# A decoder layer on one Trainium2 core: the value projection as two Strassen passes, with keys and queries projected first

## The chip, the cores and the metric

The kernel runs on one core of a Trainium2 chip. The core has a matrix engine (PE, with PEld for its weight loads), a vector engine (DVE), a scalar engine (ACT), a general engine (POOL) and a sequencer for transfers (SP). The metric is the device time of one execution in microseconds. The kernel before took 2018.26 us in the median of three runs (2017.77 to 2018.28).

## The reference

One layer of a decoder trunk, 512 tokens by 2048 features, all in float32, and a final norm:

```
h = rmsnorm(x, ln_mix)
sb_q, sb_k, sb_v, sw_q, sw_k, sw_v = split(h @ w_in)        # w_in: 2048 x 4608
sb_o = stick_breaking_attention(sb_q, sb_k, sb_v)           # 16 heads of 64, strictly causal
sw_o = sliding_window_sink_attention(sw_q, sw_k, sw_v, sinks, slopes)   # 16 query heads, 4 key heads, window 128
x = x + concat(rmsnorm(sb_o), rmsnorm(sw_o)) @ w_out
gate, up = split(rmsnorm(x, ln_ffn) @ w_gate_up)            # 2048 x 2*5632
x = x + (silu(gate) * up) @ w_down
return rmsnorm(x, ln_final)
```

Stick-breaking attention has no softmax. Its weight is exp(log sigmoid(z) + the sum of log sigmoid(-z') over the keys between), for keys before the query. The value projection sb_v is h (512 x 2048) times a 2048 x 1024 part of w_in.

## The kernel before

A float32 product is made of three matmuls of rounded operands (float32r): high by high, low by high and high by low, where the low part is what rounding left. So each weight tile that arrives is split into a high part (a copy on ACT, `whi`) and a low part (a subtraction on DVE, `wlo`), and so are the activations.

**The queue.** Everything up to the second output projection is made from one list, `queue`. An entry (slab) names its sources, a prep function and its matmuls in groups of three. `step()` (L226) runs one group; at group 2 of a slab it also loads the next two slabs and splits the next one. `drain(mark)` (L264) steps up to a mark. `pull(ns)` (L254) steps until a budget is used up: a group of three 512-column matmuls counts 648, one of three 256-column matmuls 324; what a pull lacks or has too much is carried to the next one in `carry`, which is never reset. `defer(n, fn)` calls a function n steps later. The slabs cost about the same: 8 groups of 648, or 16 of 324. Buffers for raw weights (`RAWB`) are three, for split weights two.

**The order.** The first 16 slabs are the value projection, `add_v(0)` and `add_v(1)`: two halves of 512 columns, each 8 slabs of two row blocks. While the first half runs, x arrives in 20 pieces; the slabs' prep transposes it (`h_make`, two row blocks of 128 features a slab) and splits it into `h_hi` and `h_lo`. The transposes write tile z, the first half's sums tiles m and o (two PSUM banks each), the second half's tile z (four banks). `x_squares` and `rstd1_make` form the norm's factor, which is applied as the sums leave PSUM; the values go to `vst`, split again.

Then come 32 slabs of stick-breaking queries and keys (`add_qk(u)` for eight pairs of heads, four slabs each), 8 slabs of window keys and first window queries (`C_SWK`, `C_SWQ`, kept in `kq`), and 4 of window values (`add_swv`). They are the fill of the stick-breaking stage: 66 iterations over 64 jobs (16 heads by four key blocks), in each of which the stage's own small matmuls alternate with three pulls of `SBFILL / 3`, where `SBFILL` is 30 slabs over 62. `sb_begin(h)` drains the queue up to the slabs of its pair of heads, three jobs ahead. The marks leave the last slab of the window values outside the loop (`sb_mark = swv_end - 1`), and what the loop left over is drained behind it. Within an iteration the jobs overlap: the logarithm of job j (three ACT instructions, L614 to L616), the suffix sums of job j-1 (matmuls L661 to L664), its exponential (L669), the copy of job j's high part (L624), and the weighted sum of job j-2 (L684, L685). The weighted sum of a head takes one of the two o banks and is folded on ACT and DVE (L511, L513); every second head its square is added on POOL (L520, L521). The two factors of the output norms are made by `sumsq_rstd`, which takes another o bank.

The window attention (16 jobs, 18 iterations) follows with 12 more query slabs, of which the first group uses the two o banks, and 16 slabs of the first output projection as its fill, one slab's worth per iteration.

**What orders instructions.** A planner places the instructions of each engine, in general by the program's order, but an instruction whose inputs are ready can be placed ahead of one that waits. Those called through `pV`, `pA`, `pG`, `pT` and `dma` stay in program order among themselves on their engine.

**The down projection**, much later, already runs as ten passes of Strassen's scheme in the variant of Winograd: `class Pass`, with seven block products instead of eight, each in two slots of 12 matmuls, POOL making the differences of weight blocks, ACT two copies of each (`hp` into PSUM for the subtraction, `whi`), DVE the low part and the sums out of PSUM. A table of slots, `plan`, says in which slot each load, sum and copy is issued.

## Time and profile before

| | |
|---|---|
| median of three runs | 2018.26 us |
| span of the profiled execution | 2015.3 us |
| its own time | not listed apart from the span |
| PE busy | 2002.2 us (99%) |
| DVE, ACT, POOL busy | 1453.2, 1455.7, 1031.9 us |
| PE's share of the chain that ended last | 97% |

A row of a group reads: line, engine, operation, tiles (out<-in), shapes, count, then busy time, mean duration of one in ns, and the engine's idle time before them with what ended it. Matmuls are pipelined, so their listed duration is longer than their spacing. A row of a timeline reads: start in us, duration, engine, line, operation, and how many are merged. A row of windows gives the stretch, its length, and for PE, PEld, DVE, ACT and POOL the busy time and count, then the granted clock of PE, the DMA share and GB/s.

### The profile page before, as it was taken

How to read it: one execution, taken by the hardware profiler on the slowest of the kernel's cores; microseconds unless marked ns; L12 is line 12 of the kernel's file. 1: busy time of each engine (PE TensorE's matmuls, PEld its weight loads, DVE VectorE, ACT ScalarE, POOL GpSimd, SP SyncE). 2: the span in 40 equal slices, each digit the busy share in tenths (PEclk: the TensorE clock that was granted, in tenths of full speed). 3: DMA queues.
4: the chain of work that ended last, by engine and by line, in shares of the span. 5: the costliest groups of instructions: out<-in, count | busy, mean ns of one | idle time of the engine just before them, and what ended most of it. 6: DMA issues, size and time to landing. Idle time of an engine off the chain costs nothing.

```text
span 2015.3 us, 29246 instructions
## 1 busy us (share of the span) xinstructions
PE 2002.2 (99%) x10412; PEld 1707.3 (85%) x10412; DVE 1453.2 (72%) x1968; ACT 1455.7 (72%) x2009; POOL 1031.9 (51%) x562
## 2 busy tenths in 40 slices
PE   9999999999999999999999999999999999999998
PEld 8888888898788888888888888888888888888886
DVE  4358888768963777777777777777777867767767
ACT  5347777657842477777777777777777788788787
POOL 0014444300100066766667666666766778878883
PEclk9999999999999999999999999999999999999999
DMA  5332222222343354453544535444454743533523
GB/s 192 92 93 65 64 66 71 63 84 67 103 147 114 120 157 125 111 141 101 136 116 120 137 101 140 112 124 132 104 141 106 266 157 111 180 128 106 175 86 115
DMA packets 286369, 240.23 MB, mean 119 GB/s; under 512 B 11024, under 2 KB 237392, under 8 KB 283792
## 3 DMA queue, kind: packets, MB, share of 16 engines
q1 hardware_dynamic: 285552, 235.71, 39.6%
q8 instruction: 82, 1.34, 0.3%
q0 software_dynamic: 288, 1.32, 0.2%
q10 hardware_dynamic: 384, 1.34, 0.2%
q14 instruction: 63, 0.52, 0.1%
HBM read 218.40 MB, written 19.92 MB: 118 GB/s over the span
## 4 chain that ended last, share of the span: by engine, by line
PE 97%; DVE 1%; ACT 1%; issue 0%; DVEq 0%; POOL 0%; ACTq 0%; POOLq 0%
PE o L118 34%; PE m L118 28%; PE m L390 4%; PE m L391 4%; PE m L392 4%; PE m L359 2%; PE m L358 2%; PE m L360 2%; PE o L360 2%; PE o L359 2%; PE o L358 2%; PE z L118 1%; PE z L359 1%; PE z L360 1%; PE z L358 1%; PE z L853 1%
## 5 line engine op out<-in xcount | busy, mean ns | idle before, releaser
L118 POOL TENSOR_TENSOR t<-raw,t 128x1024 f32<-128x1024 f32 x107 | 272.6, 2548 | 277.5 <-ACT hp L118 263.3
L118 DVE TENSOR_TENSOR wlo<-t,hp 128x1024 fp32r<-128x1024 f32 x235 | 286.5, 1219 | 172.3 <-PE o L118 107.5
L118 ACT ACTIVATE whi<-t 128x1024 fp32r<-128x1024 f32 x235 | 249.3, 1061 | 123.1 <-PE o L118 74.7
L118 PE MATMUL o<-hca,whi 128*128 128x512 f32 x880 | 307.5, 391 | 0.0
L118 POOL TENSOR_TENSOR t<-raw,raw 128x1024 f32<-128x1024 f32 x106 | 275.3, 2601 | 16.0 <-issue 10.3
L118 DVE TENSOR_TENSOR wlo<-raw,hp 128x1024 fp32r<-128x1024 f32 x175 | 213.6, 1221 | 81.3 <-issue 50.5
L118 ACT ACTIVATE whi<-raw 128x1024 fp32r<-128x1024 f32 (+1 forms) x177 | 187.1, 1057 | 99.8 <-PE m L118 72.0
L118 PE MATMUL o<-hca,wlo 128*128 128x256 f32 x880 | 244.0, 280 | 0.0
L118 ACT ACTIVATE hp<-t 128x1024 fp32r<-128x1024 f32 x235 | 236.9, 1008 | 0.0
L220 DVE TENSOR_TENSOR wlo<-raw,whi 128x1024 fp32r<-128x1024 f32 x103 | 126.5, 1228 | 137.7 <-ACT whi L219 135.0
L219 ACT ACTIVATE whi<-raw 128x1024 fp32r<-128x1024 f32 x103 | 108.7, 1056 | 152.2 <-PE o L360 75.4
L118 PEld LDWEIGHTS o<-hca,whi 128*128 128x128 f32 x880 | 164.2, 187 | 35.8
L118 PE MATMUL m<-hca,whi 128*128 128x512 f32 x528 | 186.3, 392 | 1.1 <-DVE hca L118 1.1
L118 ACT ACTIVATE hp<-raw 128x1024 fp32r<-128x1024 f32 x179 | 180.8, 1010 | 3.1 <-DVE wlo L118 2.2
L118 PEld LDWEIGHTS o<-hca,wlo 128*128 128x128 f32 x880 | 165.6, 189 | 0.4
L390 PE MATMUL m<-hhi,whi 128*128 128x512 f32 x384 | 156.3, 407 | 0.0
L391 PE MATMUL m<-hlo,whi 128*128 128x512 f32 x384 | 150.5, 392 | 0.0
L392 PE MATMUL m<-hhi,wlo 128*128 128x512 f32 x384 | 150.4, 392 | 0.0
L118 PE MATMUL m<-whi,dca 128*128 128x512 f32 x592 | 146.9, 389 | 0.0
L118 PE MATMUL o<-whi,dca 128*128 128x512 f32 x592 | 146.8, 389 | 0.0
L118 PE MATMUL m<-hca,wlo 128*128 128x256 f32 x528 | 146.3, 280 | 0.0
L118 PEld LDWEIGHTS o<-whi,dca 128*128 128x128 f32 x592 | 111.1, 188 | 23.1
(351 smaller groups left out, 5143.6 us busy)
## 6 DMA issues: line engine op xcount, KB each, us to landing
raw<-in_w_gate_up_dram SPq DMA_DIRECT2D x348, 256.0 KB, 5.2
raw<-in_w_down_dram SPq DMA_DIRECT2D x68, 512.0 KB, 4.8
raw<-in_w_in_dram SPq DMA_DIRECT2D x39, 512.0 KB, 3.5
raw<-in_w_in_dram SPq DMA_DIRECT2D x66, 256.0 KB, 3.3
raw<-in_w_out_dram SPq DMA_DIRECT2D x32, 512.0 KB, 3.8
aT<-w SPq DMA_DIRECT2D x44, 256.0 KB, 3.5
xd<-aT SPq DMA_DIRECT2D x10, 1024.0 KB, 7.1
rx<-in_w_down_dram SPq DMA_DIRECT2D x20, 512.0 KB, 5.7
```

The source lines that it names most:

```text
L118: return lambda *a, **k: tc.keep_in_program_order(fn(*a, **k))
L219: A.activation(out=hi, in_=raw, func=AF.Copy)
L220: V.tensor_tensor(out=lo, in0=raw, in1=f(hi), op=ALU.subtract)
L358: mm(o, lhsT=lh[:, sl], rhs=hi[:, j, :], start=first, stop=False, skip_group_check=halves)
L359: mm(o, lhsT=lh[:, sl], rhs=lo[:, j, :], start=False, stop=False, skip_group_check=halves)
L360: mm(o, lhsT=ll[:, sl], rhs=hi[:, j, :], start=False, stop=(k == nslab * a - 1), skip_group_check=halves)
L390: mm(o, lhsT=wh, rhs=xh, start=(k == 0), stop=False)
L391: mm(o, lhsT=wh, rhs=xl, start=False, stop=False)
L392: mm(o, lhsT=wl, rhs=xh, start=False, stop=(k == KT - 1))
L853: nc.tensor.transpose(out=pb[:, hh * P:(hh + 1) * P], in_=B.s[hh // 2][:, hh % 2, j * P:(j + 1) * P], identity=ident)
```

## The change

The value projection h (512 x 2048) times 2048 x 1024 is made by two passes of the seven-product scheme, one for each half of the 2048 features (16 row blocks; four blocks of h of 256 tokens by 512 features, four of the weights of 512 by 512). `class Block` takes over what the down passes' `Pass` did, and `ValuePass` derives from it. Each product sums into two banks; `take` adds them into `vacc` in SBUF. As left operands the products 1, 2 and 4 use the `h_hi` and `h_lo` that exist; for 7, 6, 5 and 3 combinations of h are formed, from `hf`, the sum of both parts, which POOL now makes in `h_make`. The forms `diff`, `s1`, `s2` and `s4` run on POOL, their high parts on ACT, their low parts on DVE.

The eight slabs of window keys and first window queries move to the front of the queue, where x arrives (`add_kq`: four m and o banks, each slab's weights as two pieces of 256 columns; in slab 0 four). The x row blocks are prepared in the order of `KTS`, the last ones a slab sooner. At slab 5 the phase's memory is handed to the value passes, whose first loads and sums are issued between the remaining groups (slots -6 to -1). After slot 27 come the slabs 8 to 10 of stick-breaking queries, and the values are scaled and split out of `vacc` in deferred steps. The stick-breaking stage keeps its rate of pulling, but the eight slabs are no longer in its queue. Before the first window scores the drain up to `smarks[0]`, which was zero, becomes a pull of 16000.

```diff
-    def open_phase(name, bufs):
+    def open_phase(name, bufs, **kw):
...
         if i == 0:
             for j in range(a):
-                dma(out=raw[:, j, :], in_=srcs[0][j * P:(j + 1) * P, :])
+                for k, src in enumerate(srcs):
+                    dma(out=raw[:, j, k * n:(k + 1) * n], in_=src[j * P:(j + 1) * P, :])
...
         split_scaled(pb, gcol[:, kt:kt + 1], h_hi[kt], h_lo[kt])
+        if kt % 4 == 0:
+            h8s.append((h8[0], h8[1]))
+            hf.append(v8.tile([P, 4, 512], F32, tag="v8", name="hf"))
+        pG.tensor_tensor(out=hf[kt // 4][:, kt % 4, :], in0=f(h_hi[kt]), in1=f(h_lo[kt]), op=ALU.add)
...
+    PD = ("1", "7", "6", "4", "5", "2", "3")
+    class Block(Weights):
+        def __init__(self, d, g, c0, u, fresh):
+            Weights.__init__(self)
+            self.d, self.g, self.c0, self.u, self.fresh = d, g, c0, u, fresh
+            self.raw, self.t, self.bank = {}, {}, {}
+        def difference(self, p, i, t):
+            a, b = {"7": ("22", "12"), "5": ("12", "11"), "6": ("22", "T5"), "4": ("21", "T6")}[p]
+            self.t[p, i] = t
+            pG.tensor_tensor(out=t, in0=self.raw[a, i], in1=self.t[b[1], i] if b[0] == "T" else self.raw[b, i],
+                             op=ALU.subtract)
+        def src(self, pi):
+            p, i = pi
+            return self.t[pi] if pi in self.t else self.raw[{"1": "11", "2": "21", "3": "22"}[p], i]
+        def product(self, pi):
+            p, i = pi
+            if i == 0 and p in "1752":
+                get = (pm, po)[(self.d + (p in "72")) % 2]
+                self.bank[p] = [get(), get()]
+            on = {"6": "1", "4": "7", "3": "5"}.get(p)
+            bk = self.bank[on or p]
+            hi, lo = self.hi.pop(pi), self.lo.pop(pi)
+            for half, w in ((0, hi), (1, hi), (0, lo)):
+                for e in range(2):
+                    for t in range(2):
+                        pT.matmul(bk[t], lhsT=self.left(p, 2 * i + e, half, t * P), rhs=w[:, e, :],
+                                  start=(on is None and i == 0 and half == 0 and w is hi and e == 0),
+                                  stop=(w is lo and e == 1), skip_group_check=True)
...
-    vst = [v8.tile([P, 16, P], F32R, tag="v8", name="vst") for _ in range(NT)]
+    vst = [None] * NT
-    def add_v(c):
...
+    KTS = ((), (2, 3), (4, 5), (6, 7), (8, 9, 10), (11, 12, 13), (14, 15), ())
...
+    def add_kq():
...
         def prep(s):
-            if c == 0:
-                h_make(2 * s)
-                h_make(2 * s + 1)
-                if s == 7:
-                    defer(1, lambda: [x_squares(k) for k in range(3)])
-                    defer(2, lambda: [x_squares(k) for k in range(3, 5)])
-                    defer(4, rstd1_make)
-                    defer(11, rstd1_rows)
-        add_tok(lambda s: win[s * 256:(s + 1) * 256, C_SBV + c * 512:C_SBV + (c + 1) * 512],
-                8, 2, 512, hT, lambda: four(1 - c), v_done, prep)
+            for kt in KTS[s]:
+                h_make(kt)
+            for c in {3: (0, 1), 5: (2,), 6: (3,)}.get(s, ()):
+                x_squares(c)
+        for s in range(8):
+            order = [(c, j) for c in range(4) for j in range(2)] if s == 7 else [(c, j) for j in range(2) for c in range(4)]
+            rows = slice(s * 256, (s + 1) * 256)
+            queue.append(dict(srcs=[win[rows, C_SWK:C_SWK + 256], win[rows, C_SWQ:C_SWQ + 256]], a=2, b=512, big=None,
+                              mms=[one(c, j, s) for c, j in order], post=None,
+                              pre=(lambda: bk.update(b=four(1))) if s == 0 else None, prep=lambda s=s: prep(s)))
...
+    class ValuePass(Block):
...
+    vp = [ValuePass(g) for g in range(2)]
+    for g in range(2):
+        b0, u = 14 * g, vp[g]
+        for k, q, i in ((-6, "12", 0), (-6, "22", 0), (-5, "11", 0), (-4, "12", 1), (-3, "22", 1), (-2, "11", 1),
+                        (0, "21", 0), (1, "21", 1)):
+            at_slot(b0 + k, "load", u.load, q, i)
+        for k, p, i in ((-3, "7", 0), (-2, "5", 0), (-1, "7", 1), (0, "5", 1), (1, "6", 0), (2, "6", 1),
+                        (3, "4", 0), (4, "4", 1)):
+            at_slot(b0 + k, "sum", u.sum, p, i)
+        for k, fn, *args in ((-5, u.diff), (-5, u.s1), (-4, u.s2), (-4, u.form, "7", "h"), (-3, u.form, "7", "l"),
+                             (0, u.form, "6", "h"), (1, u.form, "6", "l"), (4, u.form, "5", "h"), (5, u.form, "5", "l"),
+                             (5, u.s4), (7, u.form, "3", "h"), (8, u.form, "3", "l")):
+            at_slot(b0 + k, "late", fn, *args)
+        for k, p in enumerate(PD):
+            at_slot(b0 + 2 * k + 2, "take", u.take, p)
+    for k in range(3):
+        at_slot(14 + (7, 9, 11)[k], "late", vp[1].add_v, k, pG)
...
-    add_v(0)
-    add_v(1)
+    add_kq()
...
-    NV = len(queue)
-    drain(NV - 2)
-    open_phase("sbp", 1)
+    def drain_to(slab, group):
+        while pos[0] < slab or pos[1] < group:
+            step()
+    def value_slot(n):
+        run(n, "load")
+        run(n, "sum")
+        vof(n + 1, "to_hi")
+        vof(n + 1, "to_lo")
+        vof(n + 2, "to_hp")
+    drain_to(5, 3)
+    x_squares(4)
+    defer(4, rstd1_make)
+    open_phase("vp", 1, reuse_waits="tile")
+    for n in range(-6, 0):
+        if n == -2:
+            open_z("psv")
+        value_slot(n)
+        if n == -1:
+            vacc[:] = [o8.tile([P, 4, 512], F32, tag="o8", name="vacc") for _ in range(2)]
+            vu.append(phase[1].tile([P, 2, 512], F32, tag="vu", name="vu", bufs=1))
+        while pos[0] * 8 + pos[1] < 64 + 4 * (n + 1):
+            step()
+        run(n, "late")
     for u in range(8):
         add_qk(u)
-    def kq_done(c, pb):
-        if kq[0] is None:
-            kq[0] = const.tile([P, 4, 512], F32, tag="swv", name="kq")
-        k_evac(pb, kq[0][:, c, :])
-
-    add_feat(win, [(C_SWK, 256)], two_m, kq_done)
-    add_feat(win, [(C_SWQ, 256)], two_m, lambda c, pb: q_evac(pb, kq[0][:, 2 + c, :]))
+    for n in range(28):
+        value_slot(n)
+        if n == 24:
+            load(8)
+        if n == 27:
+            load(9)
+            split(8)
+        vof(n, "product")
+        run(n, "take")
+        run(n, "late")
+    run(28, "take")
+    open_z("psw")
+    def value_split(c, t):
+        if vst[t] is None:
+            vst[t] = v8.tile([P, 16, P], F32R, tag="v8", name="vst")
+        bv = vacc[c][:, t, :].rearrange("p (h d) -> p h d", d=HD)
+        split_scaled(bv, rs1["c"][:, t:t + 1], vst[t][:, c * 8:(c + 1) * 8, 0:HD],
+                     vst[t][:, c * 8:(c + 1) * 8, HD:P])
+    for t in (3, 2, 1, 0):
+        value_split(0, t)
+    def kq_scale():
+        for c in range(4):
+            (k_evac if c < 2 else q_evac)(kq[0][:, c, :], kq[0][:, c, :])
+    defer(3, rstd1_rows)
+    defer(8, lambda: [value_split(1, t) for t in (3, 2, 1, 0)])
+    defer(14, kq_scale)
+    open_phase("sbp", 1)
+    drain_to(11, 0)
+    oA = [o8.tile([P, 4, 512], F32, tag="o8", name="oA") for _ in range(2)]
     add_swv()
...
-    drain(smarks[0])
+    pull(16000.0)
     at(swa_scores, 0)
...
-    class Pass(Weights):
+    class Pass(Block):
...
-    nc = _bacc.Bacc("TRN2", target_bir_lowering=False, num_devices=1)
+    nc = _bacc.Bacc("TRN2", target_bir_lowering=False, num_devices=1, dynamic_dma_scratch_size=8192)
```

190 lines of the change are left out of this document (116 added, 74 removed).

## The prediction

> **What bounds the kernel now.** I read the page first: its busy shares, its forty slices and its chain of work that ended last.
>
> ```profile
> span 2015.3 us, 29246 instructions
> PE 2002.2 (99%) x10412; PEld 1707.3 (85%) x10412; DVE 1453.2 (72%) x1968; ACT 1455.7 (72%) x2009; POOL 1031.9 (51%) x562
> PE   9999999999999999999999999999999999999998
> PEclk9999999999999999999999999999999999999999
> PE 97%; DVE 1%; ACT 1%; issue 0%; DVEq 0%; POOL 0%; ACTq 0%; POOLq 0%
> ```
>
> PE is busy in every slice at full clock, and the chain is PE's own work for 97% of the span. A matmul taken away is therefore worth its spacing, as long as PE is fed elsewhere. A matmul's spacing isn't its listed duration (389 ns), because matmuls overlap. It comes from start times, so I asked next for the matmuls of the second half of the value projection (they alone write tile z at lines 358 to 360), and for the chain in the down passes, which already run the class that the change reuses.
>
> ```profile
> L358 PE MATMUL z<-whi,hhi x64: 389/389/393, 58.8 to 101.6; 128*128 128x512 f32 x64
> L360 PE MATMUL z<-whi,hlo x64: 389/389/389, 59.2 to 102.1; 128*128 128x512 f32 x64
> 1972.86 5.44 PE m L118 x24
> 60.00:100.00 40.00, 40.00 (x178) 33.14 (x177) 10.88 (x10) 8.95 (x10) 0.00 (x0) 1.00 0.32 93
> 1602.94:1983.75 380.81, 380.81 (x1682) 315.32 (x1681) 276.85 (x294) 310.63 (x320) 303.64 (x123) 1.00 0.38 130
> ```
>
> The 192 matmuls of that half start from 58.8 to 102.1 us: 43.3 / 191 = 0.227 us each. A down pass gives 24 in 5.44 us, also 0.227. The last row (busy time by window: PE, PEld, DVE, ACT, POOL) covers all ten down passes: PE never idles while ACT is busy 82%, POOL 80% and DVE 73%. So 2.72 us a slot is a pace that this code holds.
>
> **The change, part by part.**
>
> *Matmuls removed.* The value projection has 2 halves x 16 row blocks x 4 x 3 = 384 matmuls of 512 columns; two passes of 14 slots with 12 each make 336. 48 x 0.227 = **-10.9 us**. The key/query slabs keep their 192 matmuls and only move from the fill of the stick-breaking stage to the front. This term has a firm end: nothing else that PE does is removed.
>
> *The front.* The first slabs now bring their weights in more pieces. The first and second columns of the next rows are the start and the time over all merged DMA issues on SP's queue.
>
> ```profile
> 0.81 1.80 SPq L100 DMA_DIRECT2D xt<-in_x_dram  x4
> 2.66 0.91 SPq L100 DMA_DIRECT2D raw<-in_w_in_dram  x2
> 3.61 1.86 SPq L100 DMA_DIRECT2D xt<-in_x_dram  x4
> 13.54 3.04 SPq L100 DMA_DIRECT2D xt<-in_x_dram  x4
> 7.32 0.73 PE L358 MATMUL m<-whi,hhi 128*128 128x512 f32 x2 [0.19 <-ACT whi L118]
> 9.27 1.03 PE L118 MATMUL z<-ident,xt 128*128 128x128 f32 x8
> 34.56 1.03 PE L118 MATMUL z<-ident,xt 128*128 128x128 f32 x8
> 40.89 1.03 PE L118 MATMUL z<-ident,xt 128*128 128x128 f32 x8
> ```
>
> An issue takes 0.46 us (1.86 / 4). Slab 0 gets four instead of two, so the next piece of x goes out 0.9 us later, and each later slab has one issue more, ahead of the x pieces queued behind it. PE reached the transposes of that piece at 9.27 us. Between 0 and 0.9 us are lost there; I take **+0.3**, since the bytes ahead of it are the same. The last x pieces went out by 16.6 us, or 18 with the added issues. Some are wanted a slab sooner now, and a slab takes 6.3 us (34.56 to 40.89): at 34.6 instead of 40.9 us. So no more is lost there. The value passes' loads, 16 of 512 KB as before, come behind slab 7's in SP's queue; a load that waits there for the memory of an x piece holds up only other value loads.
>
> *Pass 0's start.* POOL gets 16 sums of 128x512 (hf), then diff, s1, s2 and the block differences, all pinned in one order. The last h is made during slab 5, near 45 us; 11 sums of 128x1024 lie from there to the last one that product 4 needs.
>
> ```profile
> L118 POOL TENSOR_TENSOR t<-raw,ty 128x1024 f32<-128x1024 f32 x20 | 53.2, 2660 | 15.0 <-DVE wlo L118 15.0
> L118 POOL TENSOR_TENSOR t<-raw,t 128x1024 f32<-128x1024 f32 x20 | 48.6, 2431 | 4.3 <-DVE wlo L118 3.8 <-PE o L118 0.3
> L220 DVE TENSOR_TENSOR wlo<-raw,whi 128x1024 fp32r<-128x1024 f32 x29 | 35.4, 1221 | 7.1 <-ACT whi L219 6.7
> 370.27 1.29 POOL L521 TENSOR_TENSOR sqA<-sqA,oc 128x512 f32<-128x512 f32 x1
> ```
>
> The transposes at 40.89 (rows above) are those that slab 5 will now make for the last two blocks, some 0.9 us later; with ACT, DVE and a 1.29 us POOL sum the last hf ends near 45.8. 11 x 2.43 gives 72.5, 11 x 2.66 gives 75.1. Slot 0 starts near 58 (the same 192 matmuls and 64 transposes as before), slot 7 at 58 + 7 x 2.72 = 77.0, and ACT's two copies (about 1.05 us each) must come before it: wanted by 74.9. The slack lies between 2.4 and -0.2 us, and the first sum may also wait for the x pieces whose memory it takes over, until their squares are done. I take **+0.5**, bounds 0 and 2.7, one sum.
>
> [...]
>
> *Inside the passes*: 0. Per slot ACT has two copies, DVE one subtraction and one PSUM add, POOL at most one sum, as in the down passes. That work is covered by 2.72 us of PE; without cover it would be a rival (below). The tails of the passes hand over to slab 8, loaded at slot 24 and split at slot 27: 0.
>
> *The stick-breaking stage loses its fill.* It pulls fill slabs at a fixed rate: 30 slabs over 62 of its 66 iterations. Before, 28 query/key slabs were followed by 8 key/query slabs and 3 of four value slabs of the window part. The 8 now are gone. Adding the kernel's own costs (648 a group, 324 in the value slabs): before, 24.6 us of fill stood unused at the end; after, the queue is dry in iteration 59 and 16.6 us of what was asked for isn't there. So 6.6 iterations run bare.
>
> ```profile
> L602 PE MATMUL z<-maskb,identb x64: 229/229/230, 129.1 to 382.5; 128*128 128x128 bf16 x64
> 160.00:350.00 190.00, 190.00 (x960) 157.59 (x959) 163.68 (x283) 147.83 (x300) 84.95 (x121) 1.00 0.22 65
> L624 ACT ACTIVATE h<-e 128x384 fp32r<-128x384 f32 x14 | 7.3, 525 | 8.2 <-DVE e L623 8.2
> L615 ACT ACTIVATE e<-e 128x384 f32<-128x384 f32 x14 | 7.2, 513 | 0.0
> L616 ACT ACTIVATE e<-e,ones 128x384 f32<-128x384 f32 x14 | 8.6, 612 | 0.2
> L669 ACT ACTIVATE e<-z 128x384 f32<-128x384 f32 x15 | 7.1, 475 | 0.4 <-PE z L664 0.4
> L614 ACT ACTIVATE e<-z 128x384 f32<-128x384 f32 x14 | 6.7, 482 | 4.1 <-PE z L602 4.0
> ```
>
> With fill an iteration lasts (382.5 - 129.1) / 63 = 4.02 us. 30 x 8 / 62 = 3.9 fill groups of three matmuls are 2.64 us of it, and, with the groups that due marks force, some 2.75; so the stage's own PE work is about 1.25. Bare, the order of the ACT instructions (three for the logarithm, the weight's exponential, the copy of the high part) sets the pace: 0.48 + 0.51 + 0.61 + 0.48 + 0.53 = 2.6 us at the width 384, somewhat less over the four widths, and the head's last copies bring it back to 2.6. PE idles 2.6 - 1.25 = 1.35 us, times 6.6 = 8.9 us.
>
> Not all of it need stay empty, since instructions that aren't pinned are placed where they are ready.
>
> ```profile
> 11.43 0.40 ACT L335 ACTIVATE xt<-xt 128x256 f32<-128x256 f32 x1
> 430.92 0.40 PE L390 MATMUL o<-hhi,whi 128*128 128x512 f32 x1
> 432.53 0.28 PE L358 MATMUL m<-whi,hhi 128*128 128x256 f32 x1
> 406.24 0.28 PE L358 MATMUL m<-whi,hhi 128*128 128x256 f32 x1
> 406.35 0.28 PE L359 MATMUL m<-wlo,hhi 128*128 128x256 f32 x1
> L511 ACT ACTIVATE oc<-o 64x512 f32<-64x512 f32 x14 | 8.3, 596 | 2.1 <-PE o L685 1.2 <-POOL af L645 0.7
> L513 DVE TENSOR_TENSOR oA<-o,oc x14: 669/683/685, 171.1 to 381.5; 64x512 f32<-64x512 f32 x14
> L520 ACT ACTIVATE oc<-oA 128x512 f32<-128x512 f32 x6 | 3.7, 624 | 0.0
> 392.55 0.44 PE L685 MATMUL o<-l,vst 128*128 128x384 f32 x1 [0.38 <-DVE l L675]
> ```
>
> The squares at 11.43 us stand behind slab 7 in the program; and PE ran query groups (430.92, tile o) ahead of value groups that are earlier in the queue (432.53, tile m). So the last value slab, which the loop itself may not pull, can move into the hole: 48 matmuls at 0.12 us (406.24 to 406.35) are 5.8 us, and 3.1 stay. After it the next fill needs both o banks. The last head's is free 0.60 + 0.68 = 1.3 us after its last weighted sum; 12 matmuls (2.7 us) can then run. The other serves the sum of squares, which needs a square (0.62), a POOL sum (1.29) and PE besides, and is free after some 4.6 us. That leaves 1.3 + 0.6 = 1.9 us open that fill covered before. 3.1 + 1.9 = **+5.0**, less the 0.4 us that PE waited there already (392.55): **+4.6**. Bounds: 0 if more fill moves in, 8.9 if none does, and 18 if a bare iteration is no shorter than a filled one.
>
> *What follows.* The debt of 16.6 us is carried, so the pull of 16 before the first window scores pulls 32.6 us of fill; that covers the stacking of keys and queries as the 24.6 us did. The window part then has 29 - 6.3 - 18 = 4.7 slabs over at its end instead of 11, 25 us to hide its last steps. I count 0.
>
> ```profile
> 500.00:550.00 50.00, 49.22 (x254) 40.06 (x253) 48.37 (x124) 43.69 (x112) 3.93 (x3) 1.00 0.34 110
> ```
>
> Here DVE is busy 48.4 of 50 us and PE waits 0.8; the shifted fill can change that by about 1 us either way. [...]
>
> *Sum*: -10.9 + 0.3 + 0.5 + 4.6 = **-5.5 us** on the profiled span of 2015.3, so 2009.8. The median of the runs, 2018.3, lies 3.0 above that span (what is around it); so I forecast **2012.8 us**. From 2.5 to 8 us of gain, 2010 to 2015.5, is this case's own range.
>
> **The rivals.**
>
> *The hole fills.* Besides the value slab, query slabs move in as well, or the chain is shorter than 2.6 us. Then only the front costs: -10.9 + 0.8 - 0.4 + 1 = -9.5, **2008.8**. For it speaks the reordering shown; against it the two o banks.
>
> *Nothing moves in.* The static order leaves the value slab behind the stage, where it then covers the o banks: -10.9 + 0.8 - 0.4 + 8.9 = -1.6, **2016.7**. For it: from 160 to 350 us PE never showed a gap that a planner had to fill, so its model of a bare iteration is untested.
>
> *Bare iterations are no faster* (slower than before). DVE was busy 163.7 of 190 us and ACT 147.8 with the fill's splits included; if waits between engines, not fill, made the 4.02 us, 6.6 iterations leave 6.6 x 2.77 = 18.3 us: -10.9 + 0.8 - 0.4 + 18.3 = +7.8, **2026.1**. Without reordering it turns slower once a bare iteration exceeds 1.25 + 10.5 / 6.6 = 2.84 us; against it, the ACT sum of 2.6.
>
> *The passes don't hold 2.72 us a slot*, since key/query evacuations, the statistics and pass 0's forms meet on ACT. At 3.1 us the 28 slots give back 10.6: **2023.4**. Against it: ten passes without a gap at 82% of ACT.
>
> **How the numbers follow.** Forecast 0.42, hole filled 0.20, nothing moved 0.22, bare iterations slow 0.08, passes slow 0.08. About 0.2%, 4.0 us, is what a measurement can tell here: faster means below 2014.2, slower above 2022.3. The forecast lies there with about three quarters (0.31), the filled hole with all of it: faster 0.51. Slower gets most of the last two, 0.15; the rest, 0.34, is no change. The range runs from the whole 10.9 (2007.4) up over the third case and half way to the slow ones: 2007 to 2021.
>
> **What would show it.** Matmuls fewer by 48; the value projection ends at 102.1 us before, near 58 + 76.2 + 0.5 = 134.7 after, with eight key/query slabs already done. In the passes, 24 matmuls per 5.44 us on m and o. In the stick-breaking stage, the spacing of the mask matmul (line 602) at 4.0 us until the thirteenth head, then near 2.6, with PE idle 5 us in all over the last seven iterations and the following five microseconds; 256-wide matmuls of the last value slab among them. A gap of PE in the first 60 us over 1 us, idle slots in the passes, or an iteration spacing that stays at 4 would each prove me wrong, and so would a PE that shows no idle in the last iterations.

## The result and the profile after

The changed kernel takes 2032.91 us (median of 4 runs, 2032.17 to 2032.92) against 2018.19 us: a ratio of 1.0072, 95% interval 1.0058 to 1.0086. It is slower by 14.7 us; the forecast was 2012.8, faster, and the time lies above its whole range (2007 to 2021). The page of the changed kernel, with the same rows as before:

```profile
span 2031.2 us, 29381 instructions
PE 2004.4 (99%) x10364; PEld 1705.1 (84%) x10364; DVE 1505.8 (74%) x2016; ACT 1502.5 (74%) x2061; POOL 1123.3 (55%) x605
PE   9999999989999999999999999999999999999998
PEclk9999999989999999999999999999999999999999
```

The 48 matmuls are gone (10412 to 10364), yet PE is listed busy 2.2 us longer, and one slice of 51 us, the ninth (406 to 457 us), has dropped below 9 in both its busy share and its clock. A listed busy time can't tell a matmul at half clock from useful work. So I measured loss in another way, in both traces: from each start of a matmul to the next, the time less the pace of its shape (0.2275 us for 512 columns, 0.175 for 384, 0.119 for 256, 0.109 for 128, 0.039 for the mask in bf16; the median spacings in the trace before are 0.228, 0.175, 0.117, 0.109 and 0.038). A spacing below the pace counts as negative. Summed by stretch, in us, with the part that the trace shows as idle time ahead of a matmul (but for the first matmul of all):

| stretch | before | after | of it idle |
|---|---|---|---|
| 0 to 52 | 2.8 | 4.0 | 0.3 |
| 52 to 64 | 0.2 | 7.4 | 4.5 |
| 64 to 139 | 0.2 | 0.2 | 0.1 |
| 139 to 152 | 0.3 | 2.9 | 2.1 |
| 152 to 405 | 7.7 | 6.8 | 0.0 |
| 405 to 460 | 0.6 | 17.1 | 6.7 |
| 460 to 700 | 3.8 | 4.2 | 1.2 |
| 700 to the end | 3.6 | 3.5 | 1.4 |
| sum | 19.2 | 46.0 | |

26.8 us more lost less 48 x 0.2275 = 10.9 gives 15.9, the difference of the two spans (2031.2 - 2015.3). This balance closes by construction, since a loss is what a spacing leaves over its pace: it says where time went, and doesn't test the 10.9. Two of the runs below do, in which nothing is lost between 52 and 152 us: the first has the plain projection, the last the passes. This is the row with which the next slab begins, in the first and in the last run:

```profile
147.59 0.39 PE L394 MATMUL m<-hhi,whi 128*128 128x512 f32 x1
```

```profile
134.96 0.39 PE L396 MATMUL m<-hhi,whi 128*128 128x512 f32 x1
```

The 384 matmuls of the plain projection start at 59.41 us and take 87.3 (88.18 less eight 128-column matmuls between them); the 336 of the passes start at 58.80 and take 76.2. So the saving came in full, and three places gave back more.

**The stall at 53.6 us.** PE in time order: start, duration, and in brackets the idle time with what ended it.

```profile
53.60 0.39 PE L544 MATMUL m<-hlo,whi 128*128 128x512 f32 x1
58.53 0.79 PE L545 MATMUL m<-hhi,wlo 128*128 128x512 f32 x1 [4.54 <-DVE wlo L221]
59.12 0.63 PE L543 MATMUL m<-hhi,whi 128*128 128x512 f32 x1
```

PE waits 4.54 us for the low half of the last key/query slab; behind the wait each matmul lasts 0.63 us where it took 0.39. Here is what VectorE did until then, and POOL beside it:

```profile
48.21 1.83 DVE L283 TENSOR_TENSOR rt<-rr 128x4 f32<-128x4 f32 x1 [0.51 <-ACT rr L281]
50.07 0.16 DVE L284 TENSOR_TENSOR rt<-rt,rv 128x4 f32<-128x4 f32 x1
50.27 2.26 DVE L285 TENSOR_SCALAR rt<-rt 128x4 f32<-128x4 f32 x1
...
52.76 4.58 DVE L298 TENSOR_SCALAR dg<-ident,rstd 128x128 f32<-128x128 f32 x2
57.26 1.21 DVE L221 TENSOR_TENSOR wlo<-raw,whi 128x1024 fp32r<-128x1024 f32 x1
```

```profile
47.62 2.40 POOL L118 TENSOR_TENSOR t<-hf 128x1024 f32<-128x1024 f32 x1
50.10 4.86 POOL L118 TENSOR_TENSOR hf<-hf 128x1024 f32<-128x1024 f32 x2
54.92 2.33 POOL L118 TENSOR_TENSOR t<-raw,raw 128x1024 f32<-128x1024 f32 x1
57.33 3.36 POOL L118 TENSOR_TENSOR raw<-raw,rx 128x1024 f32<-128x1024 f32 x1
```

An operation on four elements a partition takes 0.16 us in one row and 1.83 or 2.26 in its neighbours. The long one that starts at 48.21 ends at 50.04, POOL's sum at 50.02. Two diagonal tiles take 4.58 us together and end at 57.34; POOL's sum from 54.92 ends at 57.25. So each of these VectorE instructions that starts while POOL's runs ends within 0.09 us of POOL's, and only the slab's low half behind them is late for PE.

**The passes' end.** Two waits of about 1 us:

```profile
141.36 2.12 PE L118 MATMUL o<-whi,vf 128*128 128x512 f32 x8 [1.04 <-ACT whi L118]
148.56 0.60 PE L299 MATMUL z<-dg,ones 128*128 128x128 f32 x3 [1.06 <-DVE dg L298]
```

```profile
139.02 1.34 ACT L272 ACTIVATE vst<-vacc,rstd 128x512 fp32r<-128x512 f32 x2 [1.70 <-POOL vacc L118]
140.26 1.04 ACT L118 ACTIVATE whi<-raw 128x1024 fp32r<-128x1024 f32 x1
```

The first two value splits, 1.34 us on ScalarE, are placed ahead of the last slot's high half, which PE needs first; the second pair of diagonals waits for the first to free its two buffers.

**The end of the stick-breaking stage.** Busy time by window (columns: length, PE, weight loads, VectorE, ScalarE, POOL, granted clock, DMA), first two rows of after, then the 34 us behind the last weighted sum of the kernel before:

```profile
416.40:435.10 18.70, 14.48 (x71) 9.74 (x69) 17.04 (x33) 15.03 (x32) 7.35 (x13) 0.94 0.00 1
435.10:447.70 12.60, 10.18 (x45) 9.02 (x45) 8.20 (x19) 3.89 (x8) 2.47 (x4) 0.55 0.01 1
```

```profile
396.00:430.00 34.00, 33.97 (x243) 31.97 (x243) 18.78 (x36) 12.41 (x23) 2.43 (x4) 1.00 0.26 78
```

At 416.4 us the fill is used up. From there to the last weighted sum at 435.07 PE loses 9.2 us, and from there to 447.70, where query slabs flow again, another 7.2, at a mean clock of 0.55. VectorE is busy 17.0 of the first 18.7 us. In the kernel before, fill still lay behind the stage, and PE had no gap and no lower clock. What stands at the end, in PE's order:

```profile
435.07 0.80 PE L924 MATMUL o<-l,vst 128*128 128x512 f32 x1 [0.38 <-DVE l L914]
...
443.27 0.58 PE L364 MATMUL m<-whi,hhi 128*128 128x256 f32 x1 [1.07 <-DVE swv L273]
...
447.70 0.50 PE L396 MATMUL o<-hhi,whi 128*128 128x512 f32 x1
```

### The profile page after: what moved, and what is told of

It is laid out like the page before. It is cut to its first block, busy times and chain, and to the rows that moved or that the text cites. A ratio compares the mean times of both kernels' runs of the same rounds, so it can differ in the third digit from the quotient of the medians.

```text
span 2031.2 us, 29381 instructions
## 1 busy us (share of the span) xinstructions
PE 2004.4 (99%) x10364; PEld 1705.1 (84%) x10364; DVE 1505.8 (74%) x2016; ACT 1502.5 (74%) x2061; POOL 1123.3 (55%) x605
## 3 DMA queue, kind: packets, MB, share of 16 engines
q8 instruction: 82, 1.34, 0.3%
q10 hardware_dynamic: 384, 1.34, 0.2%
## 4 chain that ended last, share of the span: by engine, by line
PE 74%; DVE 2%; ACT 1%; DMA 1%; issue 0%; DVEq 0%; POOL 0%; ACTq 0%; POOLq 0%
PE o L118 34%; PE m L118 28%; PE m L364 1%; PE m L366 1%; PE m L365 1%; PE o L365 1%; PE o L366 1%; PE o L364 1%; PE z L118 1%; DMA raw<-in_w_out_dram 1%; PE m L398 1%; PE m L397 1%; PE m L396 1%; DVE wlo L221 0%; PE z L1092 0%; PE o L398 0%
## 5 line engine op out<-in xcount | busy, mean ns | idle before, releaser
L118 DVE TENSOR_TENSOR wlo<-t,hp 128x1024 fp32r<-128x1024 f32 x247 | 300.9, 1218 | 180.2 <-PE o L118 108.5
L118 ACT ACTIVATE whi<-t 128x1024 fp32r<-128x1024 f32 x247 | 262.1, 1061 | 127.6 <-PE o L118 76.9
L118 POOL TENSOR_TENSOR t<-raw,raw 128x1024 f32<-128x1024 f32 x114 | 296.9, 2607 | 26.8 <-issue 11.7
L118 DVE TENSOR_TENSOR wlo<-raw,hp 128x1024 fp32r<-128x1024 f32 x187 | 228.1, 1220 | 86.0 <-issue 52.1
L118 ACT ACTIVATE whi<-raw 128x1024 fp32r<-128x1024 f32 (+1 forms) x189 | 199.6, 1056 | 104.1 <-PE m L118 74.5
L221 DVE TENSOR_TENSOR wlo<-raw,whi 128x1024 fp32r<-128x1024 f32 x87 | 109.6, 1260 | 88.1 <-ACT whi L220 87.5
L220 ACT ACTIVATE whi<-raw 128x1024 fp32r<-128x1024 f32 x87 | 91.7, 1054 | 102.8 <-PE o L366 40.2
L118 PEld LDWEIGHTS m<-whi,dca 128*128 128x128 f32 x592 | 111.0, 188 | 23.1
L396 PE MATMUL m<-hhi,whi 128*128 128x512 f32 x320 | 130.3, 407 | 0.0
L118 PE MATMUL m<-hcs,whi 128*128 128x512 f32 x352 | 125.9, 392 | 0.0
```

Of the source, the lines that this page charges most:

```text
L118: return lambda *a, **k: tc.keep_in_program_order(fn(*a, **k))
L220: A.activation(out=hi, in_=raw, func=AF.Copy)
L221: V.tensor_tensor(out=lo, in0=raw, in1=f(hi), op=ALU.subtract)
L396: mm(o, lhsT=wh, rhs=xh, start=(k == 0), stop=False)
```

## The experiments

Each run's edit is against the changed kernel, and its time stands against 2032.9; the kernel before took 2018.0 to 2018.2 us beside them. "Loss" is the sum defined above.

### The moved fill alone

The passes are taken out: keys and first queries stay in front, the value projection behind them is the plain one, without POOL's sums.

```
+    add_v(0)
+    add_v(1)
-    for n in range(28):
-        value_slot(n)
...
-        vof(n, "product")
...
```

> Edit against the changed kernel: keys and first queries are still projected while x arrives, but the value projection behind them is the plain one of the kernel before (16 slabs, no passes, no sums on POOL). It does the 48 matmuls again (+10.9). Theory (the moved fill alone opens the hole in the tail, and POOL's sums alone the stall at 53 us): 2032.9 + 10.9 - 7.4 - 2.2 (the waits at the passes' end) = 2034 (2031 to 2037), with no PE wait over 1 us before 65 us and the same hole at the end of the stick-breaking stage. Rival (the stall at 53 us comes from where the chain of rstd1 is issued, POOL or not): 2040 to 2043. Rival (the hole comes from the passes, which hand over late, and not from the moved fill): 2018 to 2022.

Measured: 2034.68 us, 1.0083 of before (1.0068 to 1.0098). Loss 0.0 us from 52 to 152, 17.4 us from 405 to 460. The theory's 2034 held in both places. So the move alone costs 16.5 us against the kernel before, and the passes, which take 10.9 us of matmuls away, bring 1.8: their preparation and end cost the rest.

### The front

**The statistics later.**

```
-    defer(4, rstd1_make)
+    at_slot(20, "late", lambda: rstd1_make())
-        V.tensor_reduce(out=sst, in_=ss1, axis=AX.X, op=ALU.add)
-        rs1["c"] = rstd_from(sst, NT, 1.0 / D, "rstd1")
+        pV.tensor_reduce(out=sst, in_=ss1, axis=AX.X, op=ALU.add)
+        rs1["c"] = rstd_from(sst, NT, 1.0 / D, "rstd1", pV, pA)
```

> Edit against the changed kernel: the chain that makes rstd1 is no longer issued four steps into the seventh slab but pinned behind slot 20 of the passes, where POOL is idle between its sums; nothing else moves. Theory (VectorE's small instructions wait for POOL's running sums, and the wait makes the last low half of the key/query slab late): the 4.5 us wait of PE at 53.6 us goes, the half clock between 58 and 64 us with it, together 7.4 us: about 2025.5 us (2023 to 2028). Rival (the low half is late because it itself runs beside POOL's sums, whatever stands ahead of it): a wait of 1 us or more stays and the clock still falls: 2030 to 2033. Rival (the chain of rstd1 only carries its wait to slot 20): a new wait of 2 us or more near 115 us and no gain, 2033.

Measured: 2031.09 us, 1.0063 (1.0046 to 1.0079): only 1.8 us gained. The stall at 53 us went, with its half clock: loss 0.0 us from 52 to 64. Two new waits took its place.

```profile
72.36 1.89 PE L118 MATMUL m<-whi,vf 128*128 128x512 f32 x7 [1.89 <-ACT whi L118]
123.48 1.89 PE L118 MATMUL o<-whi,vf 128*128 128x512 f32 x7 [1.65 <-ACT whi L118]
```

The second is inside the moved chain: ScalarE waited 4.48 us for it, since its second VectorE instruction took 2.38 us beside a POOL sum. The first is POOL's row of sums: with PE 6.9 us ahead (slot 0 at 59.43 us instead of 66.28), the difference that the fifth slot needs came 1.9 us late. The stall had hidden it. The theory was right on the cause and wrong on the gain; the rival about slot 20 held in part, with a new wait of 1.65 us instead of 2 or more.

**POOL's block sums left out.** The three sums of x for the first pass aren't made, and its form for product 7 takes a block as it stands, so that pass's values are wrong.

```
-        for k, fn, *args in ((-5, u.diff), (-5, u.s1), (-4, u.s2), (-4, u.form, "7", "h"), (-3, u.form, "7", "l"),
+        for k, fn, *args in (*(((-5, u.diff), (-5, u.s1), (-4, u.s2)) if g else ()), (-4, u.form, "7", "h"), (-3, u.form, "7", "l"),
```

> Edit against the changed kernel: the three block sums of x for the first value pass (issued five and four slots ahead of it on POOL, 2.4 us each) are left out, so that the values of that pass are wrong; all else is as in the changed kernel, the chain of rstd1 at the same place. Theory (VectorE's small instructions stretch to the end of POOL's running sum): the 128x4 instructions of the chain take under 0.5 us where they took 1.8 to 2.3, the diagonal tiles under 1 us each, and the wait of 4.5 us for the last low half shrinks below 1.5 us: 2026 to 2030. Rival (they are long because of what they wait for on their own engine): the durations stay and so does the stall: 2032 to 2033.

Measured: 2035.3 us in one run, and a wait of 6.84 us where it was 4.54. Neither side's number held (2026 to 2030 and 2032 to 2033), because POOL didn't fall idle: its later differences simply moved up. But the rows show the mechanism more cleanly than the changed kernel's. VectorE, then POOL:

```profile
48.84 1.85 DVE L283 TENSOR_TENSOR rt<-rr 128x4 f32<-128x4 f32 x1 [0.51 <-ACT rr L281]
50.92 2.25 DVE L285 TENSOR_SCALAR rt<-rt 128x4 f32<-128x4 f32 x1
53.21 2.30 DVE L287 TENSOR_TENSOR rstd<-rr,rt 128x4 f32<-128x4 f32 x1
```

```profile
48.27 2.40 POOL L118 TENSOR_TENSOR t<-raw,raw 128x1024 f32<-128x1024 f32 x1
50.74 2.40 POOL L118 TENSOR_TENSOR raw<-raw,rx 128x1024 f32<-128x1024 f32 x1
53.11 2.38 POOL L118 TENSOR_TENSOR t<-raw,raw 128x1024 f32<-128x1024 f32 x1
```

VectorE's ends are 50.69, 53.17 and 55.51; POOL's 50.67, 53.14 and 55.49. Three different instructions on 128x4 end 0.02 to 0.03 us behind POOL's. That is waiting, not slow work.

**Statistics in three parts (the mean, ScalarE's two functions, the rest), and the block sums s1 and s2 on VectorE.**

```
-    defer(4, rstd1_make)
+    at_slot(19, "late", lambda: rstd1_make(0))
+    at_slot(20, "late", lambda: rstd1_make(1))
+    at_slot(21, "late", lambda: rstd1_make(2))
...
-            pG.tensor_tensor(out=self.block("21"), in0=self.block("21"), in1=self.block("22"), op=ALU.add)
+            (pG if self.g else pV).tensor_tensor(out=self.block("21"), in0=self.block("21"), in1=self.block("22"), op=ALU.add)
```

> Edits against the changed kernel: the chain of rstd1 is issued in three parts behind slots 19, 20 and 21 of the passes, so that neither VectorE nor ScalarE waits inside it; and two of the first pass's three block sums of x are made by VectorE in place of POOL. Theory (with the chain moved whole, 1.9 us of wait came back at 70 us because POOL's row of sums is the bound at the start of the first pass, and 1.6 us at 121 us inside the chain): both waits go, the end of the passes keeps its 2 us: 2031.1 - 3.5 = 2027.6, and at best 2032.9 - 7.4 = 2025.5; 2025 to 2029. Rival (VectorE's sums, long beside POOL's, make the low halves late instead): a wait of 1 to 4 us between 50 and 70 us, 2029 to 2033.

Measured: 2030.8 us, 1.0063 (1.0046 to 1.008). The two waits went, and a wait of 2.82 us for the same low half came: the rival. Between POOL's sums four of VectorE's 128x1024 instructions in a row took 3.37 to 3.42 us instead of 1.2, the low half among them. POOL's sums beside them took 3.22 to 3.35 us instead of 2.4: moving two of the six sums that POOL makes ahead of the first pass only made both wait for each other.

**All early sums on VectorE.** The six that POOL made before slot 0 of the first pass (diff, s1, s2, and three weight differences) go there, so that POOL is idle; the chain of rstd1 stays where the change has it.

```
+                            pV if self.g == 0 and (p, i) in (("7", 0), ("5", 0), ("7", 1)) else None)
...
-            pG.tensor_tensor(out=self.s3, in0=self.block("11"), in1=self.block("21"), op=ALU.subtract)
+            (pG if self.g else pV).tensor_tensor(out=self.s3, in0=self.block("11"), in1=self.block("21"), op=ALU.subtract)
...
-            dg = sm.tile([P, P], F32, tag="dg", name="dg", bufs=2)
+            dg = sm.tile([P, P], F32, tag="dg", name="dg", bufs=4)
```

> Edits against the changed kernel: the six sums and differences that POOL makes for the first value pass before slot 0 go to VectorE (in the traces 2.4 us each on POOL, 1.2 on VectorE), and the diagonal tiles of rstd1 get four buffers in place of two. The chain of rstd1 stays where it was. Theory (an instruction of VectorE that reads and writes memory starts only when POOL's running one has ended, as in the run without the block sums, where four of them ended within 0.05 us of POOL's instructions): with POOL idle the chain's instructions take 0.2 us again, the wait of 4.5 us and the half clock behind it go, so does the wait of 1.1 us for the second pair of diagonals at 147 us: 2032.9 - 7.4 - 1.1 = 2024.4 (2023 to 2027). Rival (VectorE, with 7.3 us of sums more, makes the last low half late itself): 2027 to 2031.

Measured: 2024.96 us, 1.0034 (1.0021 to 1.0046); loss 0.0 us from 52 to 64 and from 139 to 152. The theory's 2024.4 held (its two edits, the sums and the buffers, weren't run apart); the value splits' wait at the passes' end stays (loss 1.9 us, now near 133 us).

```profile
48.72 0.16 DVE L283 TENSOR_TENSOR rt<-rr 128x4 f32<-128x4 f32 x1 [0.51 <-ACT rr L281]
49.12 0.17 DVE L285 TENSOR_SCALAR rt<-rt 128x4 f32<-128x4 f32 x1
52.81 0.28 DVE L298 TENSOR_SCALAR dg<-ident,rstd 128x128 f32<-128x128 f32 x1
60.20 1.58 DVE L298 TENSOR_SCALAR dg<-ident,rstd 128x128 f32<-128x128 f32 x1
```

The instruction of 1.83 us takes 0.16, that of 2.26 takes 0.17, a diagonal 0.28. The fourth diagonal confirms it: from 59.29 to 61.69 POOL makes a sum again, and that one diagonal takes 1.58 us and ends at 61.78. VectorE, with 7.3 us of sums more, was no bound: it does each in 1.2 us, half of POOL's 2.4.

### The end of the stick-breaking stage

**A tile of their own for the window values.**

```
-                swv[0] = const.tile([P, NT, 4, P], F32R, tag="swv", name="swv")
+                swv[0] = own[0].tile([P, NT, 4, P], F32R, name="swv")
```

> Edit against the changed kernel: the window values get a tile of their own, opened between the passes' pool and the stick-breaking pool, in place of the tile that the keys and queries hold until they are stacked. Theory (the last value slab is stuck behind that tile and holds the split buffers, so the fill behind it starts only at 447 us): its last 24 matmuls (24 x 0.216 = 5.2 us) run inside the hole of 416 to 443 us and the query slabs follow sooner, 4 to 9 us gained: 2024 to 2029. Rival (the last head's chain through VectorE and ScalarE sets the end of the stage, and what fills the hole does not matter): the hole shrinks in PE idle time but the first window scores come no sooner: 2031 to 2034.

Measured: 2033.18 us, 1.0075 (1.006 to 1.009); loss 16.9 us from 405 to 460 and the same wait for swv at the end. My theory of the stuck tile fell. In the trace VectorE is busy from 434 to 443 us, but for some 1.2 us, mostly with the last head and the stacking, and the values' instructions come behind them at 442.9.

**The clock held up.**

```
+            for _ in range(n):
+                pT.matmul(zb[:, 256:384], lhsT=ones, rhs=ones, start=True, stop=True, skip_group_check=True)
```

> Edit against the changed kernel: in the last 14 iterations of the stick-breaking stage two extra 128x128 matmuls of the ones tile go into an unused part of the iteration's score bank, twice an iteration where such a part exists. They compute nothing. Theory (half of the loss in the tail is the granted clock, which falls to 0.50 from 434 to 446 us because PE is sparse there): the clock stays above 0.9 and the matmuls on the last heads' chain run at full rate, 2 to 6 us gained: 2027 to 2031. Rival (the chain waits for VectorE and ScalarE, PE's rate is no part of it): the clock stays up and the time does not move or rises by up to 2 us: 2032 to 2035.

The extra matmuls open an accumulation of their own in a bank where the iteration's scores are still summed. The run's output is off by a relative 0.71, by my reading through the last heads' scores; the other work is unchanged. Measured: 2034.9 us, 1.0083 (1.0068 to 1.0098).

```profile
416.40:435.10 18.70, 17.07 (x113) 14.29 (x111) 15.87 (x32) 15.72 (x35) 9.26 (x14) 1.00 0.01 2
435.10:447.70 12.60, 8.48 (x32) 6.94 (x32) 10.72 (x21) 3.69 (x8) 2.52 (x4) 0.53 0.00 0
```

The clock stayed at 1.00 to the last iterations, and nothing came sooner (the last weighted sum at 435.8 us, 435.1 without the extra matmuls): the rival, within its 2032 to 2035. Up to there PE's rate is no bound. What half clock costs behind that point, this run doesn't tell: the extra matmuls had ended, and the clock was 0.53 there, 0.55 in the changed kernel.

**Stacking on POOL.**

```
-            stack_two(kq[0][:, c, :], e * HD, kst[c][:, 2 * e, :], kst[c][:, 2 * e + 1, :])
+            stack_two(kq[0][:, c, :], e * HD, kst[c][:, 2 * e, :], kst[c][:, 2 * e + 1, :], G)
```

> Edit against the changed kernel: the copies and differences that stack the window's keys and first queries go to POOL in place of VectorE (VectorE was busy 3.8 of 4 us from 428 to 440 us, POOL 0 to 1.3). Theory (without fill PE waits for VectorE, which has the last heads' chain and the stacking to do, so less work on VectorE ends the hole sooner): 4 to 8 us gained, 2025 to 2029. Rival (POOL's running instructions hold VectorE up as they did at 50 us, or POOL takes longer for the copies than VectorE did): no gain or up to 5 us lost, 2032 to 2038. Rival (the hole is set by fill alone, so that nothing else moves it): 2031 to 2034.

Measured: 2039.8 us, 1.0109 (1.0094 to 1.0124); 12.0 us idle from 425 to 460, up from 6.0, waiting for the stacked tiles from POOL. POOL took 1.26 to 1.70 us for a stacked half where VectorE takes 0.69. The first rival held, with 1.8 us more than its range: POOL is too slow at this work to relieve VectorE. What the stage would take with VectorE relieved and nothing else slower, no run shows.

**Two query groups as fill.**

```
+    for g in (1, 2):
+        add_feat(win, [(C_SWQ + g * 256, 256)], two_m,
+                 lambda c, pb, g=g: q_evac(pb, qraw[:, 2 * g - 2 + c, :]))
     add_swv()
```

> Edit against the changed kernel: the second and third group of window queries (8 slabs, 192 matmuls of 0.216 us, 41.5 us) are projected before the window values, as fill of the stick-breaking stage, into a raw tile of 8 KB a partition of their own; they are stacked in the window part. So that stage has as much fill again as the kernel before gave it. Theory (the 16 us lost between 410 and 460 us are the fill that the stage lacks, nothing else): PE stays full at a clock of 1.00 to the first window scores and all but 2 us come back: 2032.9 - 14.4 = 2018.5 (2016 to 2021). Rival (the chain of the last heads through VectorE is longer than before, whatever PE has beside it): 5 us or less come back: 2027 to 2033. Rival (the window part, which gives 41.5 us of fill away, runs dry in its turn): a new hole between 480 and 560 us, 2024 to 2030.

Measured: 2071.23 us, 1.0264 (1.0248 to 1.0279). The stage is whole again (loss 2.9 us from 405 to 460, against 17.1), and the window part lost 52 us between 500 and 640. Two windows, then the score matmuls with their first and last start:

```profile
410.00:450.00 40.00, 39.62 (x191) 32.42 (x190) 34.48 (x57) 26.86 (x49) 13.55 (x18) 1.00 0.22 67
...
500.00:560.00 60.00, 47.40 (x217) 37.75 (x216) 46.88 (x116) 39.42 (x100) 1.29 (x1) 0.86 0.16 53
```

```profile
L1054 PE MATMUL z<-kst,qst x64: 274/283/419, 474.2 to 636.0; 128*128 128x256 f32 x64
```

The theory held on the cause, and the last rival on where it would be lost, but not on its price: it had put 2024 to 2030. The scores began at 474 us instead of 431, behind 34 us of fill that had been queued ahead of them, and then the fill was gone while the window's own chain still ran.

**One query group as fill.**

```
+    for g in (1,):
+        add_feat(win, [(C_SWQ + g * 256, 256)], two_m,
+                 lambda c, pb, g=g: q_evac(pb, qraw[:, 2 * g - 2 + c, :]))
     add_swv()
```

> Edit against the changed kernel: as with two groups of window queries in the fill, but one (4 slabs, 96 matmuls, 20.7 us) into a raw tile of 4 KB a partition. With two groups the stick-breaking stage kept PE full to its end, but the first window scores stood behind 34 us of fill (474 us against 431) and the window part, with 41.5 us of fill less, was dry from 516 us and lost 52 us. In the changed kernel the window's own chain ends at 615 us and the fill at 644, so it has 29 us to spare, which is more than 20.7 and less than 41.5. Theory (the loss is a balance of fill between two stages that are each bound by their chains): the hole at 416 to 445 us closes but for 2 us and no new one opens: 2032.9 - 14 = 2019 (2017 to 2022). Rival (the scores stand behind the fill again, and the window chain starts too late): 2023 to 2032. Rival (the window part has nothing to spare): the gain is lost there, 2031 to 2040.

Measured: 2021.11 us, 1.0015 (1.0005 to 1.0024): 11.8 us gained.

```profile
416.40:435.10 18.70, 18.70 (x127) 17.01 (x126) 14.97 (x27) 13.93 (x27) 7.04 (x11) 1.00 0.19 58
435.10:447.70 12.60, 11.57 (x87) 10.75 (x86) 12.04 (x20) 8.40 (x14) 0.41 (x1) 1.00 0.20 53
```

The same two windows: PE is full in the first and the clock is 1.00 in both. From 405 to 460 the loss is 5.3 us, 11.8 less than in the changed kernel, and from 460 to 700 4.5 against 4.2. So half as much fill as was moved away, put back, returns 11.8 of the 16.5 us, and the window part can spare that much, not twice as much.

### Together

> Both sets of edits together: one group of window queries joins the fill of the stick-breaking stage, and the first pass's early sums go to VectorE with four buffers for the diagonal tiles. Theory (the two losses lie in different stages and add up): 2032.9 - 11.8 - 8.0 = 2013.1 (2011.5 to 2015), faster than the kernel before by 5 us. What is then left of the 10.9 us that the passes save is lost at 133 us (1.2 and its clock, a low half waits behind value splits on ScalarE) and about 440 to 450 us (3 to 4). Rival (the stick-breaking stage starts 8 us sooner, and its chain, not PE, sets the window part): under half of the sum, 2017 to 2023.

Measured: 2013.42 us (2012.9 to 2015.03), 0.9978 of before (0.9969 to 0.9987). The two losses add up, as expected to 0.3 us. The last run adds two placements to it:

```
-    rstdA = sumsq_rstd(sqA, "rstdA")
...
     pull(16000.0)
+    rstdA = sumsq_rstd(sqA, "rstdA")
...
-                     vst[t][:, c * 8:(c + 1) * 8, HD:P])
+                     vst[t][:, c * 8:(c + 1) * 8, HD:P], A if c else pA)
```

> As the run with both sets, with two more edits: ScalarE's first four value splits stand pinned behind the passes' last high halves instead of being placed ahead of them, and the sum of squares of the stick-breaking output is turned into its scale behind three slabs of fill instead of ahead of them (its tile moves to the pool of the raw queries). Theory (each of the two waits of 1.1 to 1.2 us is a placement of one instruction and goes with it): 2 to 3 us less than the run with both sets: 2010.5 (2009 to 2013). Rival (each wait only passes to what comes next, the low halves on VectorE at 135 us and the last head's chain at 440 us): the same as the run with both sets within 1 us.

Measured: 2009.58 us (2009.03 to 2010.66), 0.9959 of before (0.9945 to 0.9972), with a span of 2007.8. No loss is left from 52 to 152 us. The first rows of its page, and the window at the end of the stick-breaking stage:

```profile
span 2007.8 us, 29383 instructions
PE 1992.2 (99%) x10364; PEld 1700.0 (85%) x10364; DVE 1503.0 (75%) x2022; ACT 1502.7 (75%) x2061; POOL 1109.2 (55%) x599
```

```profile
405.00:445.00 40.00, 38.76 (x280) 36.11 (x279) 35.25 (x69) 25.72 (x48) 11.09 (x15) 1.00 0.22 67
```

The page lists PE busy 10.0 us less than before the change (2002.2), and in the window PE idles 1.2 of 40 us at full clock. This kernel does what the change set out to do and keeps 7.5 us of the 10.9 on the span; it is the fastest of all that ran.

## Why the prediction was wrong

**Held: -10.9.** 48 matmuls fewer, at the pace they had: 76.2 us for the passes against 87.3 for the plain projection, where neither loses anything. **Held too: 0 inside the passes.** From 64 to 139 us the loss is 0.2 us, as before, at 2.72 us a slot up to the last four; the rival of passes at 3.1 us is out.

**Just missed: the front, +0.3, bounds 0 and 0.9.** It measured 1.2 (4.0 against 2.8 up to 52 us). No run took it apart.

**Failed: "Pass 0's start", +0.5, bounds 0 and 2.7.** It measured 7.2. I had followed POOL's chain to what POOL feeds and asked when its sums would be there. That part was sized about right: once the stall was gone, a difference came 1.9 us late, inside the bounds. What I had not asked is what POOL's running sums do to VectorE, which at that time carried the statistics, the diagonals and the low half PE needed next. I had priced what runs beside a POOL sum for POOL's chain alone, as 2.43 or 2.66 us a sum. The traces show what it did to VectorE: ends within 0.09 us of POOL's in the changed kernel and within 0.03 in the run without the block sums, 0.16 us turning into 1.83 to 2.30.

The profile before already held it, behind the mean of 2.66 us that I read. Of those 20 sums 15 took 2.40 to 2.43 us and five 3.39 to 3.41, each of the five beside a VectorE sum of two SBUF tiles that took 2.26 to 2.35 us itself. First the row of all 20 (shortest, median and longest in ns), then one of the five with VectorE's instructions around it:

```profile
L118 POOL TENSOR_TENSOR t<-raw,ty x20: 2401/2416/3412, 1602.8 to 1949.9; 128x1024 f32<-128x1024 f32 x20
1678.08 2.35 DVE L118 TENSOR_TENSOR dca<-xd,dca 128x1024 fp32r<-128x1024 f32 x1
1679.31 3.39 POOL L118 TENSOR_TENSOR t<-raw,ty 128x1024 f32<-128x1024 f32 x1
1680.35 1.21 DVE L118 TENSOR_TENSOR wlo<-rx,hp 128x1024 fp32r<-128x1024 f32 x1
```

The stall counts 1.6 times over, 7.2 for 4.5 idle, because the granted clock is 0.50 behind it, up to 64.2 us. The prediction had the granted clock at 1.00 throughout and no term for its fall.

**Failed: "hand over to slab 8 ... 0".** 2.6 us. The value splits and the scale's diagonals were unpinned work of the kernel before, done elsewhere; I counted their cost as hidden without naming where they would be placed. Four buffers for the diagonals removed one wait, pinning the first four splits the other.

**Failed: "The stick-breaking stage loses its fill", +4.6, bounds 0 to 18.** It measured 16.5. Of its parts:
- The dry point was right, at 416.4 us, and the pace somewhat too fast. 6.6 iterations at 2.6 us would be 17.2; to the last weighted sum it took 18.7. The weighted sums of the last seven jobs start at 416.5, 419.7, 421.8, 422.3, 426.7, 430.2 and 435.1: 3.1 us apart in the mean, but 3.5 to 4.9 for the last three. With one group of fill put back the last seven are 4.0 apart. So bare iterations do run faster than filled ones, and the rival of bare iterations no faster, though nearest in time, is out by its mechanism: it put 18.3 us of loss there, and 9.2 were measured.
- "48 matmuls ... 5.8 us": only 24 moved in ahead of the last weighted sum, and even with them the loss to there is 9.2 us, against the 8.9 I had before that subtraction. That these two agree is chance: a slower pace and 24 matmuls more offset each other.
- The "+1.9" for the o banks is the step that was most too small: 7.2 us from there to the next query slab. I had looked at two banks. By the trace VectorE was the queue that mattered: it was busy 17.0 of 18.7 us with the last heads and the stacking, and the stacking came before the values' and the splits' turn. Then PE worked through what there was at a granted clock of 0.55. That fill closes the hole is shown by two runs; how much of it is VectorE's doing is read from the trace only.
- The rival "Nothing moves in" put the whole at 2016.7. Its neighbour, in which almost nothing moves in and VectorE holds the hand-over as well, had no place among them.

**"What follows ... I count 0"** held for the changed kernel (460 to 700: 3.8 and 4.2), and the two runs with more fill show why it deserved a price: the window part can give up 20.7 us of fill and not 41.5.

The forecast's 2012.8 isn't far from the 2013.4 of the run with both sets of edits. That is no support for its terms, since that run has more fill in the stage; but it shows what the forecast left out: it took the two places at which the change would need repairs as though they had been made. By the terms as measured, 1.2 + 7.2 + 2.6 + 16.5 = 27.5 less 10.9, less 0.9 won back from 152 to 405 us, and 0.3 more behind 460, is 16.0, against 15.9 on the span.

## What to carry to other kernels

Work that runs as fill in a stage bound by its own chain is not free to move: count what the stage still needs to its last instruction, and what the next one can lend it, before pricing the gain elsewhere. When sums go to POOL, ask first what VectorE must deliver to PE in the same microseconds; if anything, let VectorE make the sums, here in half the time (1.2 us against 2.4). Look at the single durations behind a mean before pricing by it. Add the half clock behind a wait of PE to its price (here 2.82 us idle cost 4.6 and 4.54 cost 7.4), and look for placements (an unpinned instruction ahead of the one PE waits for) at every hand-over.

## What the hardware showed that I had not expected

**Some of VectorE's instructions and POOL's sums waited for each other's end, others did not.** 0.16 us became 1.83 to 2.30, and it went both ways: POOL's sum of 2.33 to 2.40 us took 3.36 at 57.33 us, where VectorE's low half of 1.21 us had started at 57.26. Held were the instructions on SBUF alone that the rows above show, those with two tiles and those with one and a constant or a column (L285, L298). Not held was the sum along rows ahead of them (L345), which took 0.18 us at 47.32 us while POOL made a sum until 47.67. Nor were the passes' low halves, which read one of their two sources, `hp`, from PSUM: the `wlo<-rx,hp` of the kernel before at 1680.35 us, the last row above, took 1.21 us in the middle of POOL's sum, and with the early sums on VectorE one took 1.21 us at 61.70 us, beside a POOL sum of 2.42 us from 61.66.

**The clock fell after waits of 2.82 and 4.54 us, and was back only after 3.4 and 6.8.** After 4.54 us idle the granted clock was 0.50 from 57.37 to 64.20 us. After 2.82 us, in the run with the statistics in three parts, it was halved too:

```profile
53.49:56.90 3.41, 0.64 (x3) 0.19 (x1) 3.41 (x3) 0.00 (x0) 3.41 (x2) 1.00 0.00 0
56.90:60.31 3.41, 3.36 (x8) 2.69 (x9) 3.41 (x2) 0.60 (x1) 3.33 (x2) 0.50 0.00 0
```

After 1.89 and 1.65 us, in the run with the statistics later, it stayed at 1.00. At the end of the changed kernel's stick-breaking stage it fell with no single wait over 1.19 us, and was 0.50 from 432.84 to 446.49 us. The second of these two stretches of the changed kernel ends with the fall; the first, as sparse, does not:

```profile
429.00 0.41 PE L900 MATMUL z<-ah,neg 128*128 128x384 f32 x1 [1.19 <-DVE e L862]
```

```profile
426.01:429.43 3.42, 2.12 (x13) 1.82 (x13) 3.33 (x7) 2.17 (x4) 1.24 (x2) 1.00 0.02 5
429.43:432.84 3.41, 2.10 (x7) 0.87 (x6) 3.25 (x6) 3.11 (x7) 0.00 (x0) 1.00 0.00 0
```

So the stretch ahead of a fall needn't be idle throughout: PE is listed busy for 0.03 of the 3.41 us before 57.37 in the changed kernel, for 0.64 and for 2.10 in the rows above. A stretch with 2.12 us busy had no fall behind it, so a limit can't be read from these runs.
